# Column means of an 8192 x 8192 array: loads of 64 KB runs issued by GpSimd, and the last pieces through the SyncE queue

## Chip, cores and metric

One core of one Trainium2 chip. The metric is the device time of one execution in microseconds (us); lower is better.

## The reference

```python
"x": np.random.randn(8192, 8192).astype(np.float32)

def reference(x):
    return np.mean(x, axis=0)
```

268.4 MB are read once and 32 KB are written.

## The kernel before

Each row tile is 128 rows of 32 KB, one row per partition. One contiguous run of a load is called a descriptor here; the trace has one packet record for each (8064 of 32 KB for the 63 full tiles). TensorE multiplies it by a column of 1/8192, so that PSUM collects the column sums. Four row groups of 32 partitions in each of four PSUM banks hold the 16 blocks of 512 columns. The last 128 rows come in smaller pieces, so that little is left to do after the last byte.

```python
ld = tile_pool(name="ld", bufs=5)
for ri in range(n_rt - 1):                      # 63 tiles of 128 rows
    t = ld.tile([P, N], f32)
    nc.sync.dma_start(out=t[:], in_=x[ri * P:(ri + 1) * P, :])
    for b in range(NB):
        for q in range(4):
            c = (b * 4 + q) * F                 # F = 512
            mm(b, q, 0, F, t[:, c:c + F], ri == 0, False)
for b in range(NB - 1):                         # last 128 rows: three pieces of 1 MB
    t = lastp.tile([P, 4, F], f32, name=f"last{b}")
    nc.sync.dma_start(out=t[:], in_=x_v[r0:r0 + P, b])
    # 4 matmuls, copy from PSUM, store through ScalarE's queue
for s in range(F // SPL):                       # and four of 256 KB, runs of 512 B
    t = lastp.tile([P, 4, SPL], f32, name=f"lasts{s}")
    nc.sync.dma_start(out=t[:], in_=x_v[r0:r0 + P, b, :, s * SPL:(s + 1) * SPL])
    # 4 matmuls of 128 columns; after the last piece one copy and one store
```

## Time and profile before

| | before |
|---|---|
| time, median | 634.28 us |
| first input packet starts | 1.74 us |
| last input packet ends | 628.35 us |
| span (first to last instruction) | 632.6 us |

The rows in the middle are from the trace's packet records, which give each descriptor's queue, start, duration and size, but not its transfer engine. What is said of one engine is matched by time: 99% of the records of 32 KB, after the first 16, start within 4 ns of the end of another packet. The 626.6 us between them are a solid stream; 4.2 us follow it. The prediction shows the lines for this. Two more lines of the page matter later: the engines' busy times with their numbers of instructions, and the queue through which the core fetches its own instructions (packets, MB, share of the 16 engines).

```profile
PE 363.6 (57%) x2072; PEld 82.7 (13%) x2072; DVE 2.9 (0%) x5; POOL 0.2 (0%) x4
...
q8 instruction: 16, 0.26, 0.2%
```

The page has two records for each matmul of the program (2072 for 1036) and as many weight loads; numbers of matmuls here are the page's unless said otherwise. There are 16 instruction fetches of 16 KB.

### The profile page before, as it was taken

To read this page: it belongs to the slowest core of one execution; us is meant where nothing else is said; L and a number is where in the kernel's file an instruction comes from. 1 tells how busy PE (TensorE), PEld (TensorE's weight loads), DVE (VectorE), ACT (ScalarE), POOL (GpSimd) and SP (SyncE) were. 2 spreads that over 40 slices of the span, in tenths; PEclk is the share of its full clock that TensorE was granted. 3 is DMA by queue.
4 is the path that set the end of the run, shared out by engine and by line. 5 is a ranking of instruction groups with operands and counts; after the bars stand their busy time and mean duration, and the time that the engine had idled before them with its cause. 6 is when DMAs were issued, how large, how long until landed. Compare 5 with 4: busy or idle time off the path is not lost.

```text
span 632.6 us, 4331 instructions
## 1 busy us (share of the span) xinstructions
PE 363.6 (57%) x2072; PEld 82.7 (13%) x2072; DVE 2.9 (0%) x5; POOL 0.2 (0%) x4
## 2 busy tenths in 40 slices
PE   1564754656547546565476554655646646556466
PEld 0111111111111111111111111111111101111111
DVE  0000000000000000000000000000000000000001
POOL 0000000000000000000000000000000000000000
PEclk9868668667786686677866778668766686687767
DMA  9999999999999999999999999999999999999996
GB/s 371 433 440 437 432 431 431 428 431 430 431 433 430 431 430 433 431 432 431 430 431 431 428 434 430 431 431 430 433 428 431 431 430 431 432 435 430 431 427 233
DMA packets 11665, 268.74 MB, mean 425 GB/s; under 512 B 1136, under 2 KB 3184, under 8 KB 3200
## 3 DMA queue, kind: packets, MB, share of 16 engines
q1 hardware_dynamic: 11616, 268.44, 99.0%
q8 instruction: 16, 0.26, 0.2%
q10 hardware_dynamic: 32, 0.03, 0.0%
q14 instruction: 1, 0.01, 0.0%
HBM read 268.44 MB, written 0.03 MB: 424 GB/s over the span
## 4 chain that ended last, share of the span: by engine, by line
DMA 87%; PE 11%; SPq 1%; issue 0%; DVE 0%
DMA t<-in_x_dram 86%; PE bank L43 11%; DMA lasts<-in_x_dram 1%; SPq L76 1%; SPq L55 0%; DVE r L79 0%
## 5 line engine op out<-in xcount | busy, mean ns | idle before, releaser
L43 PE MATMUL bank<-t,ones 128*32 128x512 f32 x2016 | 359.8, 880 | 265.1 <-DMA t<-in_x_dram 265.1
L43 PEld LDWEIGHTS bank<-t,ones 128*32 128x32 f32 x2016 | 81.2, 153 | 542.5 <-DMA t<-in_x_dram 310.8
L70 DVE COPY r<-bank 128x512 f32<-128x512 f32 x3 | 2.1, 692 | 625.3 <-PE bank L43 625.3
L43 PE MATMUL bank<-last,ones 128*32 128x512 f32 x24 | 2.7, 592 | 0.0
L43 PE MATMUL bank<-lasts,ones 128*32 128x128 f32 x32 | 1.5, 279 | 0.5 <-DMA lasts<-in_x_dram 0.5
L43 PEld LDWEIGHTS bank<-last,ones 128*32 128x32 f32 x24 | 0.7, 110 | 2.2 <-issue 1.9
L43 PEld LDWEIGHTS bank<-lasts,ones 128*32 128x32 f32 x32 | 0.8, 109 | 1.6 <-DMA lasts<-in_x_dram 1.3
L79 DVE COPY r<-bank 128x512 f32<-128x512 f32 x1 | 0.7, 692 | 1.1 <-PE bank L43 1.1
L95 POOL MEMSET const-bfloat16-1.0<- 128x1 bf16 x1 | 0.1, 102 | 0.0
L95 POOL MEMSET const-uint8-127<- 128x1 uint8 x1 | 0.1, 102 | 0.0
L95 POOL MEMSET const-float32-0.0<- 128x1 f32 x1 | 0.1, 99 | 0.2 <-issue 0.2
L95 POOL MEMSET const-float32-1.0<- 128x1 f32 x1 | 0.1, 99 | 0.0
L39 DVE MEMSET ones<- 128x32 f32 x1 | 0.1, 85 | 0.8 <-PEq L95 0.8
## 6 DMA issues: line engine op xcount, KB each, us to landing
t<-in_x_dram SPq DMA_DIRECT2D x63, 4096.0 KB, 43.1
last<-in_x_dram SPq DMA_DIRECT2D x3, 1024.0 KB, 45.3
lasts<-in_x_dram SPq DMA_DIRECT2D x4, 256.0 KB, 19.1
out_dram<-r ACTq DMA_DIRECT2D x4, 8.0 KB
```

What stands on the lines that cost most here:

```text
L39: nc.vector.memset(ones[:], 1.0 / M)
L43: nc.tensor.matmul(out=banks[b][32 * q:32 * q + 32, c0:c0 + w], lhsT=ones[:], rhs=rhs, start=start, stop=stop, tile_position=(0, 32 * q), ...
L70: nc.vector.tensor_copy(out=r[:], in_=banks[b][:])
L76: nc.sync.dma_start(out=t[:], in_=x_v[r0:r0 + P, b, :, s * SPL:(s + 1) * SPL])
L79: nc.vector.tensor_copy(out=r[:], in_=banks[b][:])
L95: nc = _bacc.Bacc("TRN2", target_bir_lowering=False, num_devices=1)
```

## The change

The intent is to halve the number of descriptors: two neighbouring rows per partition make runs of 64 KB. GpSimd issues the loads of the first 31 tiles, each declared a single packet. The last 8 MB come in four pieces through SyncE's queue. The last 512 columns are summed by four matmuls of 128 columns into a PSUM tile of their own, so that the final copy is short.

```diff
-    for ri in range(n_rt - 1):
-        t = ld.tile([P, N], f32)                                   # bufs=5
-        nc.sync.dma_start(out=t[:], in_=x[ri * P:(ri + 1) * P, :])
-        # 16 matmuls of 512 columns
+    xt = x.rearrange("(t p j) c -> t p j c", p=P, j=2)
+    for ti in range(n_t - 1):                                      # 31 tiles of 256 rows
+        t = ld.tile([P, J, N], f32)                                # bufs=3
+        nc.gpsimd.dma_start(out=t[:], in_=xt[ti], single_packet=True)
+        for j in range(J):          # 15 matmuls of 512 columns and 4 of 128 ("edge")
+            sums(t, j, range(NBLK + 1), ti == 0 and j == 0, False)
-    # last 128 rows: 3 pieces of 1 MB, 4 of 256 KB
+    t = ld.tile([P, J, N], f32)
+    cuts = [(0, 8), (8, 12), (12, 15), (15, 16)]                   # blocks of 512 columns
+    for lo, hi in cuts:
+        nc.sync.dma_start(out=t[:, :, lo * F:hi * F], in_=xt[n_t - 1, :, :, lo * F:hi * F])
+    for lo, hi in cuts:
+        for j in range(J):
+            sums(t, j, range(lo, hi), False, j == J - 1)
+        # copies from PSUM and stores through ScalarE's queue, as before
```

(The store code and the index arithmetic are cut.)

More of the change, by code (lines that the diff above doesn't have):

```diff
@@ L27 @@
     F = 512
-    NB = N // (4 * F)
-    n_rt = M // P
-    SPL = 128
-    ld = ctx.enter_context(tc.tile_pool(name="ld", bufs=5))
-    lastp = ctx.enter_context(tc.tile_pool(name="lastp", bufs=1))
+    J = 2
+    NBLK = N // F - 1
+    W = F // 4
+    n_t = M // (P * J)
+    xt = x.rearrange("(t p j) c -> t p j c", p=P, j=J)
+    ld = ctx.enter_context(tc.tile_pool(name="ld", bufs=3))
     sg = ctx.enter_context(tc.tile_pool(name="sg", bufs=1))
@@ L39, with mm @@
     nc.vector.memset(ones[:], 1.0 / M)
-    banks = [psp.tile([P, F], f32, name=f"bank{b}") for b in range(NB)]
-    def mm(b, q, c0, w, rhs, start, stop):
+    banks = [psp.tile([P, F], f32, name=f"bank{b}") for b in range(4)]
+    edge = psp.tile([P, W], f32, name="edge")
+    def mm(dst, q, rhs, first, last):
         nc.tensor.matmul(
-            out=banks[b][32 * q:32 * q + 32, c0:c0 + w],
+            out=dst[32 * q:32 * q + 32, :],
             lhsT=ones[:],
             rhs=rhs,
-            start=start,
-            stop=stop,
+            start=first,
+            stop=last,
             tile_position=(0, 32 * q),
@@ L51, in mm @@
         )
-    for ri in range(n_rt - 1):
-        t = ld.tile([P, N], f32)
-        nc.sync.dma_start(out=t[:], in_=x[ri * P:(ri + 1) * P, :])
-        for b in range(NB):
-            for q in range(4):
-                c = (b * 4 + q) * F
-                mm(b, q, 0, F, t[:, c:c + F], ri == 0, False)
-    r0 = (n_rt - 1) * P
-    out_v = out.rearrange("(b q c) -> b q c", b=NB, q=4)
-    x_v = x.rearrange("r (b q c) -> r b q c", b=NB, q=4)
-    for b in range(NB - 1):
-        t = lastp.tile([P, 4, F], f32, name=f"last{b}")
-        nc.sync.dma_start(out=t[:], in_=x_v[r0:r0 + P, b])
-        for q in range(4):
-            mm(b, q, 0, F, t[:, q, :], False, True)
-        r = resp.tile([P, F], f32, name=f"r{b}")
-        nc.vector.tensor_copy(out=r[:], in_=banks[b][:])
-        nc.scalar.dma_start(out=out_v[b], in_=r[0:128:32, :])
@@ L72, with sums @@
-    b = NB - 1
-    r = resp.tile([P, F], f32, name=f"r{b}")
-    for s in range(F // SPL):
-        t = lastp.tile([P, 4, SPL], f32, name=f"lasts{s}")
-        nc.sync.dma_start(out=t[:], in_=x_v[r0:r0 + P, b, :, s * SPL:(s + 1) * SPL])
-        for q in range(4):
-            mm(b, q, s * SPL, SPL, t[:, q, :], False, s == F // SPL - 1)
-    nc.vector.tensor_copy(out=r[:], in_=banks[b][:])
-    nc.scalar.dma_start(out=out_v[b], in_=r[0:128:32, :])
+    def sums(t, j, blocks, first, last):
+        for i in blocks:
+            if i < NBLK:
+                mm(banks[i // 4], i % 4, t[:, j, i * F:(i + 1) * F], first, last)
+            else:
+                for q in range(4):
+                    c = i * F + q * W
+                    mm(edge, q, t[:, j, c:c + W], first, last)
@@ new lines @@
+    for ti in range(n_t - 1):
[10 more added lines that the diff above has]
+            sums(t, j, range(lo, hi), False, j == J - 1)
+        if hi <= NBLK:
+            for b in range(lo // 4, (hi + 3) // 4):
+                n = min(hi - 4 * b, 4)
+                r = resp.tile([P, F], f32, name=f"r{b}")
+                nc.vector.tensor_copy(out=r[:32 * n, :], in_=banks[b][:32 * n, :])
+                o = out[b * 4 * F:(b * 4 + n) * F].rearrange("(q c) -> q c", q=n)
+                nc.scalar.dma_start(out=o, in_=r[0:32 * n:32, :])
+        else:
+            r = resp.tile([P, W], f32, name="redge")
+            nc.vector.tensor_copy(out=r[:], in_=edge[:])
+            o = out[lo * F:hi * F].rearrange("(q c) -> q c", q=4)
+            nc.scalar.dma_start(out=o, in_=r[0:P:32, :])
```

## The prediction

> **What bounds the kernel now.** I read the page's row of slices first, then its chain, then the groups of instructions and the DMA issues, and last the end of the timeline.
>
> ```profile
> DMA  9999999999999999999999999999999999999996
> GB/s 371 433 440 437 432 431 431 428 431 430 431 433 430 431 430 433 431 432 431 430 431 431 428 434 430 431 431 430 433 428 431 431 430 431 432 435 430 431 427 233
> ...
> DMA packets 11665, 268.74 MB, mean 425 GB/s; under 512 B 1136, under 2 KB 3184, under 8 KB 3200
> ...
> DMA t<-in_x_dram 86%; PE bank L43 11%; DMA lasts<-in_x_dram 1%; SPq L76 1%; SPq L55 0%; DVE r L79 0%
> ...
> L43 PE MATMUL bank<-t,ones 128*32 128x512 f32 x2016 | 359.8, 880 | 265.1 <-DMA t<-in_x_dram 265.1
> ...
> t<-in_x_dram SPq DMA_DIRECT2D x63, 4096.0 KB, 43.1
> ```
>
> The transfer engines are busy in all forty slices and move some 431 GB/s in nearly every one; only the first (371) and last (233) fall short. The 11% for matmuls in the chain is no limit: the chain steps through TensorE because a free buffer lets the next load be issued, but each load has 43.1 us from issue to landing while one load's own share is 4.19 MB / 431 GB/s = 9.7 us. Four loads stand queued ahead of it, so a late release starves nothing. TensorE waits 265.1 us for loads.
>
> The end, from the timeline:
>
> ```profile
> 628.83 0.42 PE L43 MATMUL bank<-lasts,ones 128*32 128x128 f32 x8 [0.27 <-DMA lasts<-in_x_dram]
> 629.32 0.69 DVE L79 COPY r<-bank 128x512 f32<-128x512 f32 x1 [1.07 <-PE bank L43]
> 630.04 0.52 ACTq L80 DMA_DIRECT2D out_dram<-r  x1
> ```
>
> The last piece lands at about 628.8; eight matmuls, one copy and the store bring the span to 632.6, so the tail is 632.6 - 628.4 (last input packet, from the packet records) = 4.2 us. The first input packet starts at 1.7 us. Thus span = 1.7 (start) + 626.6 (transfer stream) + 4.2 (tail), and the timed 634.28 is 1.7 us above the span.
>
> Inside the 626.6 us I used the trace's packet records: each descriptor has its own record, and on one engine the next starts as the last ends. Start-to-start spacing, median: 32 KB 1213 ns (x504 per engine), 8 KB 309 ns (x24), 512 B 24 ns (x128), completion write 6 ns (x70). Sum: 611.4 + 7.4 + 3.1 + 0.4 = 622.3 us. The other 4.3 us are the slow first packets (1.8 to 2.1 us each), the 0.26 MB of instruction fetches and scattered stalls (the mean 32 KB spacing is 1218, not 1213). The slope between 8 KB and 32 KB is (1213 - 309) / 24576 B = 36.8 ps/B, that is 435 GB/s over 16 engines. What is left at 32 KB is 1213 - 32768 x 0.0368 = about 8 ns per descriptor (5 ns at 512 B). So the pure byte time of 268.4 MB is 617 us, and all that descriptor size can still win in the bulk is 504 x 8 ns = 4.0 us.
>
> [...]Before, issue at 0.73 and first packet at 1.7, 1.0 us; nothing in this trace shows the GpSimd path.
>
> **The change part by part.**
>
> *Descriptors of 64 KB.* Of 32 tiles of 8 MB, 31 go with 8 descriptors of 64 KB per engine: 248 per engine instead of 496 of 32 KB. If every descriptor still costs 8 ns: 248 x (65536 x 0.0368 + 8) = 248 x 2418 = 599.6 us. [...]Before, the same bytes took 496 x 1213 = 601.6 us. Gain 2.0 to 3.8 us.
>
> *Last tile in four pieces, two rows per partition.* Runs of 16, 8, 6 and 2 KB, 16 descriptors of each per engine: 16 x (611 + 309 + 234 + 83) = 19.8 us with the same slope plus 8 ns. Before, the same 256 rows took 8 x 1213 + 7.4 + 3.1 = 20.2 us. Gain 0.4 us, since 2048 runs of 512 B vanish. Completion writes fall from 70 to 35 per engine: 0.2 us.
>
> *GpSimd writes descriptors.* Between loads this lies beside the stream. A buffer falls free when TensorE has done 64 matmuls, about 2 x 6 us (a run of 32 is 5.0 to 6.6 us in the chain) after its tile landed; then two tiles of 19.5 us minus those 12 us are still queued, 27 us of cover. Only the first load's descriptor writing is exposed.[...]
>
> *Tail.* The last copy is 128x128 instead of 128x512 (0.69 us); an estimate is 0.3 us less. The last matmuls (eight of 128 columns) are the same number as before.
>
> Sum of the mechanism: -(2.0 to 3.8) - 0.4 - 0.2 + 1.0 - 0.3 = -1.9 to -3.7 us. A share of the scattered stalls (504 x 5 ns = 2.5 us) may go with the halved count of descriptors: about -1. That gives 629.6 to 631.4; I take 630.3.
>
> **The rivals.**
>
> *The last tile meets the GpSimd queue.* SyncE can issue its four pieces as soon as tile 28's buffer is free, about 12 us after tile 28 landed, while tile 29 is in flight and 30 is queued. If engines change queue only between packets, one small SyncE packet slips in and tile 30 still goes as one block; its 64 matmuls (11 to 13 us) then run under the last 19.7 us of pieces, and the pieces' 30 wide matmuls (30 x 0.19 = 5.7 us) just fit: 12 + 5.7 = 17.7 us. If instead 64 KB and 16 KB descriptors alternate, tile 30 lands later, with perhaps 13 us of pieces behind it or fewer; TensorE finishes 3 to 8 us after the last byte, and the time is 633 to 638. For it: engines do serve two queues at once here, since 16 KB instruction fetches took 1.0 to 1.1 us, longer than the 0.6 us of their bytes. [...]I give it one chance in five.
>
> [...]
>
> *Other read addresses.* Partitions step by 64 KB and not 32 KB. [...]A 1% loss gives 636; nothing in the profile speaks for it. One in fifteen.
>
> *All overhead goes and the start costs nothing.* 3.8 + 2.5 + 0.9 = 7.2 us less: 627. It is also nearly the floor: 617 + 1.7 + 4.2 + 1.7 = 624.6 at the slope's rate without any stall.
>
> **Range and chances.** The mechanism gives about 630 and its good end 627[...]. Faster by over 2% would be under 621.6, below that floor: 0.02. Slower by over 2% is over 647[...]: 0.05.
>
> **What would show it.** Right: slices at 432 to 434 GB/s; input descriptors of 64 KB spaced at 2410 to 2418 ns; half as many large packets; first input packet 1 us or so later; SyncE issues far before they land; last matmuls waiting for the last piece and not running behind. Wrong: a middle slice under 430 or gaps at tile borders[...]; TensorE busy without a break over the last 8 us with the last piece long landed (arbitration); slices above 435 (then the ceiling that I read from the slope is none).

The sum came to -1.9 to -3.7 us, and with about -1 for the stalls to 630.3 us. That engines change queue only between packets was the author's assumption, and the runs below show otherwise (103 packets of one queue to 106 of the other). "Two queues at once" is a reading of the fetches' duration that their starts and ends do not bear out. Of GpSimd's issues only the first stands in the chain afterwards, with 0.66 us.

## The result, and the profile after

638.75 us (637.68 to 639.12, 4 runs) against 634.4 (634.18 to 634.55, 4 runs, three of them those of the 634.28 above): ratio 1.0066, interval 1.0049 to 1.0083. By that ratio the change cost 4.2 us, where 4 us of gain were predicted.

The page after, the lines that answer to those of before: engines and instructions, slices, packets, queues, chain, issues.

```profile
PE 303.0 (48%) x2432; PEld 101.2 (16%) x2432; DVE 3.0 (0%) x6; POOL 16.7 (3%) x35
...
GB/s 391 399 458 411 441 457 408 448 407 445 453 415 441 420 436 437 433 436 432 429 436 421 449 428 436 421 440 433 428 449 411 453 415 441 424 433 442 410 415 86
DMA packets 5610, 268.79 MB, mean 422 GB/s; under 512 B 579, under 2 KB 583, under 8 KB 1110
...
q8 instruction: 19, 0.31, 0.2%
...
DMA t<-in_x_dram 75%; PE bank L47 17%; PE edge L47 2%; DVE r L83 0%; POOL t L68 0%; DVEq L116 0%; POOLq L105 0%
...
t<-in_x_dram POOLq DMA_DIRECT2D x31, 48.3
```

The packets are halved, as intended. The slices jump between 399 and 458 because a slice now counts few large packets; spread over each packet's duration, the records give 432 to 434 GB/s in every 20 us of the middle (mean 432.9), against 431 to 433 before (mean 431.2). So the bulk did get faster. The last slice is what stands out: 86 GB/s, where it was 233. The transfers end well before the kernel does. The timeline of TensorE, VectorE and ScalarE's issue near the end:

```profile
615.86 5.74 PE L47 MATMUL bank<-t,ones 128*32 128x512 f32 x27 [16.12 <-DMA t<-in_x_dram]
...
625.73 6.61 PE L47 MATMUL bank<-t,ones 128*32 128x512 f32 x56
...
632.60 0.61 PE L47 MATMUL edge<-t,ones 128*32 128x128 f32 x14
...
632.83 0.69 DVE L83 COPY r<-bank 96x512 f32<-96x512 f32 x1 [1.01 <-PE bank L47]
633.44 0.28 DVE L88 COPY redge<-edge 128x128 f32<-128x128 f32 x1
634.39 0.55 ACTq L90 DMA_DIRECT2D out_dram<-redge  x1
```

TensorE waits 16.12 us for tile 30, the last that GpSimd loads, and from 615.86 to 633.2 it doesn't wait for a transfer again: the bracket that names a wait is missing from every later group. The last input byte had landed at 627.7. SyncE's four issues stand far earlier, while tiles 29 and 30 were still moving:

```profile
578.28 2.57 SPq L75 DMA_DIRECT2D t<-in_x_dram  x4
```

In the packet records, tile 30's last 64 KB packet ended at 614.7, and by then 4.1 of the 8.4 MB of SyncE's pieces had landed. From 585 to 605 us, 103 packets of 64 KB and 106 of 16 KB started: the queues took turns, one descriptor for one.

The span splits as the prediction split it (us):

| | first input packet | stream | last byte to end | span |
|---|---|---|---|---|
| before | 1.74 | 626.6 | 4.2 | 632.6 |
| after | 2.62 | 625.1 | 9.6 | 637.3 |
| difference | +0.9 | -1.5 | +5.4 | +4.7 |

Two things had to be explained: the tail of +5.4, and why a bulk with half the descriptors gained only 1.5.

### The profile page after: what moved, and what is told of

Its sections match the earlier page's. It is cut to its first block, busy times and chain, and to the rows that moved or that the text cites. A ratio compares the mean times of both kernels' runs of the same rounds, so it can differ in the third digit from the quotient of the medians.

```text
span 637.3 us, 4993 instructions
## 1 busy us (share of the span) xinstructions
PE 303.0 (48%) x2432; PEld 101.2 (16%) x2432; DVE 3.0 (0%) x6; POOL 16.7 (3%) x35
## 4 chain that ended last, share of the span: by engine, by line
DMA 75%; PE 19%; another core or an unknown queue 4%; issue 1%; DVE 0%; POOL 0%; DVEq 0%; POOLq 0%
DMA t<-in_x_dram 75%; PE bank L47 17%; PE edge L47 2%; DVE r L83 0%; POOL t L68 0%; DVEq L116 0%; POOLq L105 0%
## 5 line engine op out<-in xcount | busy, mean ns | idle before, releaser
L47 PE MATMUL bank<-t,ones 128*32 128x512 f32 x1920 | 296.0, 738 | 330.2 <-DMA t<-in_x_dram 330.2
L47 PEld LDWEIGHTS bank<-t,ones 128*32 128x32 f32 x1920 | 87.3, 132 | 494.1 <-DMA t<-in_x_dram 314.4
L47 PE MATMUL edge<-t,ones 128*32 128x128 f32 x512 | 51.0, 277 | 0.0
L68 POOL DMA_DIRECT2D t<-in_x_dram x31 | 16.5, 532 | 542.3 <-PE edge L47 541.5
L47 PEld LDWEIGHTS edge<-t,ones 128*32 128x32 f32 x512 | 23.9, 110 | 37.7 <-issue 37.7
L83 DVE COPY r<-bank 128x512 f32<-128x512 f32 (+1 forms) x4 | 2.8, 691 | 629.9 <-PE bank L47 629.9
```

The costliest lines, as they stand in the source:

```text
L47: nc.tensor.matmul(out=dst[32 * q:32 * q + 32, :], lhsT=ones[:], rhs=rhs, start=first, stop=last, tile_position=(0, 32 * q), skip_group_ch ...
L68: nc.gpsimd.dma_start(out=t[:], in_=xt[ti], single_packet=True)
L83: nc.vector.tensor_copy(out=r[:32 * n, :], in_=banks[b][:32 * n, :])
```

## The experiments

All were timed in five rounds, except k in three. "Tail" is last input byte to end of span.

**a: the four pieces on GpSimd's queue.**

```diff
-        nc.sync.dma_start(out=t[:, :, lo * F:hi * F], ...
+        nc.gpsimd.dma_start(out=t[:, :, lo * F:hi * F], ...
```

> The last four pieces go through the GpSimd queue as well, behind tile 30. Theory T (engines take turns, one SyncE descriptor for one GpSimd descriptor, so tile 30 lands with only 13 us of transfers left while TensorE has 17 us of work): tile 30 lands some 4 MB earlier, near 605 us, TensorE waits for the last piece, tail back from 9.6 to about 4 us: 632 to 634 us. Rival R (the loss is in the stream: GpSimd descriptors or 64 KB runs let the engines drift apart): stays at 637 to 639.

634.78 us; 1.0006 of before (0.9994 to 1.0019), 4 us under the changed kernel. Tile 30 landed at 608.0 (before that only 1 MB of pieces), and the tail is 5.2 us. Its timeline:

```profile
608.56 5.77 PE L47 MATMUL bank<-t,ones 128*32 128x512 f32 x27 [9.85 <-DMA t<-in_x_dram]
...
623.33 1.92 PE L47 MATMUL bank<-t,ones 128*32 128x512 f32 x16 [1.26 <-DMA t<-in_x_dram]
...
627.02 1.49 PE L47 MATMUL bank<-t,ones 128*32 128x512 f32 x9 [1.77 <-DMA t<-in_x_dram]
```

TensorE waits for pieces again, up to the third of the four. The order of arrival was the cause of 4.4 of the 5.4 us by which the tail had grown. The time missed the expected 632 to 634 by 0.8 us: something else was still lost.

**b: without the single packet.**

```diff
-        nc.gpsimd.dma_start(out=t[:], in_=xt[ti], single_packet=True)
+        nc.gpsimd.dma_start(out=t[:], in_=xt[ti])
```

> As after, without the single packet. T: the packet flag does not hold the queue, turns are by descriptor anyway: within 1 us of after, 638 to 639.5, and the spacing of 64 KB descriptors stays 2416 to 2418 ns. If the flag held something back, SyncE's pieces now get a larger share while tile 29 and 30 are moving, and the time is 641 or more; if the flag saved per-descriptor cost, spacing rises by some ns and time by 1 to 2 us.

638.47 us (637.82 to 640.25), as with it. From 585 to 605 us 110 packets of 64 KB and 118 of 16 KB started, again in turn, and the 64 KB spacing is 2415 ns, against 2416. As used here the flag neither held the queue nor saved time.

**c: all tiles on SyncE's queue.**

```diff
-        nc.gpsimd.dma_start(out=t[:], in_=xt[ti], single_packet=True)
+        nc.sync.dma_start(out=t[:], in_=xt[ti])
```

> As after, with all tiles on the SyncE queue, 64 KB runs kept. T: order kept by the queue, TensorE not late, start 0.9 us earlier than with GpSimd: 631 to 633 us. Rival R in its form 'the 64 KB runs drift or read slower': 635 or more. This also says what 64 KB runs alone are worth against 634.4.

634.09 us; 0.9995 (0.9983 to 1.0008), which is not told apart from before. The first packet starts at 1.74 again, against 2.62 in after, so GpSimd's path costs 0.9 us once. But 631 to 633 us was missed by 1.1. The packet records say why. Each load ends with 16 completion writes (1120 records of 4 bytes for the 70 loads before), taken here as one for each of the 16 transfer engines. When all but the last 256 rows had landed (tile 30 here, the 62nd load before), these writes came on average at 604.1 us, against 606.1 before; the last of them came at 607.2, against 608.2. So the mean engine gained 2.0 us on the same bytes and the slowest 1.0. The last 256 rows then took the slowest engine 19.8 us instead of 20.2, and the last byte came 1.4 us earlier than before (627.0 against 628.3). The end of c:

```profile
626.18 1.49 PE L47 MATMUL bank<-t,ones 128*32 128x512 f32 x9 [1.80 <-DMA t<-in_x_dram]
...
627.61 0.93 PE L47 MATMUL edge<-t,ones 128*32 128x128 f32 x15
```

The matmuls of the last piece (edge) follow those of the third without a wait and end at 628.5, 1.6 us after the last byte; before it was 0.9 us (629.25 against 628.35).

**e: smaller first runs.** Same kernel as after, first piece cut into four (the copy of a bank then waits for both of its pieces; that edit isn't printed).

```diff
-    cuts = [(0, 8), (8, 12), (12, 15), (15, 16)]
+    cuts = [(0, 2), (2, 4), (4, 6), (6, 8), (8, 12), (12, 15), (15, 16)]
```

> As after (GpSimd tiles, SyncE pieces), but the first piece is cut into four with runs of 4 KB in place of 16 KB. T by descriptor turns: SyncE slips in 4 KB per 64 KB instead of 16 KB, so about 0.9 MB instead of 3 to 4 MB before tile 30 has landed; some 17 us of transfers are left then, TensorE is just in time: 633 to 635. If the engines shared by bytes or by time, 4 KB runs change nothing: 638 to 639. Rival R: 638 to 639.

635.51 us; 1.0016 (1.0004 to 1.0029). Half a microsecond above the expected window, but 3 us under the changed kernel. From 585 to 605 us, 115 packets of 64 KB and 139 of 4 KB started: still about one for one, though the bytes per turn fell to a quarter. That is a turn by descriptor, not by bytes or by time. Tile 30 landed at 609.7 after 1.9 MB of pieces, twice the 0.9 MB expected (why was not looked into), and the tail is 5.5 us.

*The second question: what holds some engines back.* A load's 16 completion writes show how far the engines have drifted apart. In the kernel before, the lags behind the first engine grow in steps: eight engines stay within 0.7 us throughout, and one engine after another of the other eight falls back by some 1.5 us. Each instruction fetch up to there starts within 4 ns of the end of a data packet and has a record of 1.0 to 1.1 us itself. As it ends (14 or 15 ns before), a data packet starts that is stretched by about 0.5 us (1680 to 1764 ns instead of 1216). Together that is 1.52 to 1.57 us for each of the 15 fetches, the size of a step. (The records name no engine; the match is by time.) Lags near the end of the bulk, and fetches up to then:

| kernel | fetches so far | lags of the slow eight, us | fetches per engine this suggests |
|---|---|---|---|
| before | 15 | one 1.6, seven 3.0 to 3.6 | 1 + 7 x 2 = 15 |
| c | 18 | six 3.0 to 3.3, two 5.0 to 5.1 | 6 x 2 + 2 x 3 = 18 |

So theory S, before the next runs: each fetch holds one engine up by 1.5 us, eight engines take them in turn, and the edge matmuls (2432 instead of 2072) brought some engines a third fetch.

**f: c without the edge matmuls.**

```diff
-            if i < NBLK:
-                mm(banks[i // 4], i % 4, t[:, j, i * F:(i + 1) * F], first, last)
-            else:
-                for q in range(4):
-                    c = i * F + q * W
-                    mm(edge, q, t[:, j, c:c + W], first, last)
+            mm(banks[i // 4], i % 4, t[:, j, i * F:(i + 1) * F], first, last)
```

The last copy then takes 32x512 of bank 3.

> c with the last 512 columns summed by one matmul like the others instead of four of 128 columns: 2048 matmuls instead of 2432, so 16 instruction fetches instead of 18 or 19. Theory S: each 16 KB fetch of instructions holds up one transfer engine by about 1.5 us, they fall in turn on eight engines, and the engine with the most fetches (three in c, lag 5.0 us) ends the stream. Then no engine has a third fetch: last input byte 1 to 1.5 us earlier than in c (627.0), time 632.6 to 633.5 with a last copy up to 0.5 us longer. Rival D (64 KB runs let the engines drift by themselves): lag of 5 us and time as in c, 634.1 or a little more.

16 fetches; largest lag at tile 30 3.5 us (15 fetches so far: seven of 3.0 to 3.5, one of 1.8). The last byte lands at 625.9, 1.1 us earlier than in c, as S has it. Yet the time is 634.29 (1.0000, 0.9988 to 1.0013), because my mended tail was worse: 6.6 us. Its end:

```profile
627.12 0.69 DVE L77 COPY r<-bank 96x512 f32<-96x512 f32 x1 [3.01 <-PE bank L46]
...
627.86 1.90 PE L46 MATMUL bank<-t,ones 128*32 128x512 f32 x4 [0.80 <-DVE r L77]
...
629.80 0.70 DVE L82 COPY redge<-bank 32x512 f32<-32x512 f32 x1 [2.00 <-PE bank L46]
```

With the edge in the same bank, the last matmuls wait for the copy of that bank (the bracket names VectorE). That is what the separate edge tile had bought.

**g: c with VectorE adding the two rows first.**

```diff
-        for j in range(J):
-            sums(t, j, range(NBLK + 1), ti == 0 and j == 0, False)
+        for k in range(4):
+            h = slice(k * 4 * F, (k + 1) * 4 * F)
+            nc.vector.tensor_add(out=t[:, 0, h], in0=t[:, 0, h], in1=t[:, 1, h])
+            sums(t, 0, range(4 * k, 4 * k + 4), ti == 0, False)
```

> c with VectorE adding the two rows of each partition in the first 31 tiles, so TensorE needs 627 matmuls instead of 2432, some 5 fetches. S: no engine has more than one fetch, largest lag about 1.5 to 2 us instead of 5.0 at tile 30, last input byte 2 to 3.5 us earlier than in c: 630.5 to 632 us. D: lag and time as in c, 634. A third possibility: VectorE's adds[...] hold buffers longer and the stream gets gaps: over 635.

632.60 us; 0.9972 (0.9960 to 0.9985): faster than both kernels. The page:

```profile
PE 220.1 (35%) x1254; PEld 35.5 (6%) x1254; DVE 278.9 (44%) x130; POOL 0.2 (0%) x4
...
q8 instruction: 10, 0.16, 0.1%
```

I had mixed two counts: 627 are the program's matmuls, which is 1254 of the page's, and so there are 10 fetches, not 5. Nine had come by tile 30, where eight engines lag by 1.1 to 1.8 us and one by 2.6. S accounts for 7 + 2 = 9 of these steps; one of the eight lags remains without a fetch (one packet at 262.1 us was stretched by 0.6 us with no fetch beside it). The last byte lands at 625.1, 1.9 us earlier than in c. The miss of 0.6 us against the expected range fits the five fetches too few in my count, since one engine got a second one; no run separates this.

**h: the changed kernel with the same adds.** Edit as in g, on the changed kernel.

> The changed kernel itself (GpSimd tiles, single packet, SyncE pieces) with the same VectorE adds. T: SyncE still takes turns, tile 30 still lands near 615, but now some 9 us of VectorE and 7 us of trailing TensorE work overlap and end by about 626, so little or nothing is late: tail about 5 us instead of 9.6; with S the stream also ends 2 to 3 us earlier: 631 to 634 us. If turns cost transfer time in themselves: 636 or more.

636.40 us; 1.0033 (1.0019 to 1.0047): a miss. The stream ended 1.4 us earlier than in the changed kernel (626.3 against 627.7), as S says, but the tail is still 8.4 us. I had counted VectorE's and TensorE's work as overlapping to the end. Its chain of waits shows that they don't:

```profile
613.77 4.50 DVE t L71 x2
618.28 0.04 issue
618.32 5.51 PE bank L47 x29
...
624.15 5.29 PE bank L47 x44
```

Tile 30 landed at 612.6; its four adds lasted from 613.77 to 622.7 (8.9 us, where some 9 were expected), TensorE could end it only after the last of them, and the pieces' matmuls followed without a wait, to 630.2. From landing to end these are again some 17 us of work against 13.7 us of transfers left, so the long tail stays. The turns themselves cost little transfer time: the stream is 0.3 us longer than g's (623.7 against 623.4).

**i and k: the kernel before with matmuls of half width,** so twice the instructions and nothing else.

```diff
-                mm(b, q, 0, F, t[:, c:c + F], ri == 0, False)
+                for h in (0, F // 2):
+                    mm(b, q, h, F // 2, t[:, c + h:c + h + F // 2], ri == 0, False)            # i
+                    mm(b, q, h, F // 2, t[:, c + h:c + h + F // 2], ri == 0 and h == 0, False) # k
```

> The kernel before with matmuls of 256 columns instead of 512 in the 63 full tiles: 4088 matmuls instead of 2072, 31 or 32 instruction fetches instead of 16, nothing else. S: up to four fetches on each of eight engines, lag 6 to 7 us instead of 3.6 before the last pieces, time 634.4 + 2.5 to 3.5 = 637 to 638. If a fetch costs only the 0.6 us of its bytes: 635.5 to 636. D: 634.4.

i took 637.38 us, but its result was wrong (relative error 0.089), which was not meant. An error of 0.088 would come of losing the first 128 of 8192 rows in half of the columns, the square root of 1/64 x 1/2 (an estimate for random input).

> i gave a wrong result, since the start flag of the second half column block undid the first half's first sum; here only the first half starts a sum. Same instruction count: S expects the same time as i, 637.4 us (3.0 over before), a largest lag near 6.7 us before the last pieces, and a right result. If i's time had to do with its error: 634 to 635.

k, whose only difference from i is the start flag of the second halves, is right and takes 637.25 us (637.21 to 637.36); 1.0047 (1.0033 to 1.0061), 3.0 us over the 634.24 of before.

```profile
PE 354.6 (56%) x4088; PEld 186.9 (29%) x4088; DVE 2.9 (0%) x5; POOL 0.2 (0%) x4
...
q8 instruction: 32, 0.52, 0.3%
```

TensorE is no busier than before (354.6 us against 363.6). With 30 fetches so far, six engines lag by 6.3 to 6.6 us and two by 4.5 to 5.0: 6 x 4 + 2 x 3 = 30. The last byte lands 2.8 us later. Two more fetches on the slowest engines at 1.5 us each are 3.0: doubling the instructions and nothing else gives the step that S asks for.

**j: g with the last store issued by SyncE.**

```diff
-            nc.scalar.dma_start(out=o, in_=r[0:P:32, :])     # of the edge
+            nc.sync.dma_start(out=o, in_=r[0:P:32, :])
```

> g with the last store (2 KB) issued by SyncE, which is idle then, instead of ScalarE, which in g is still issuing the store before it: 0.67 us lay between the end of the last copy and the issue. Expected 0.4 to 0.7 us less than g's 632.6: 632.0 to 632.2, the best so far. If the end is set by the store before the last, no change: 632.6.

632.26 us; 0.9969 (0.9955 to 0.9982). 0.34 us less than g: a little less gain than expected, and small beside the runs' spread of 0.5. It was run at another time. It is the lowest of all kernels here: 2 us under before, 6.5 under the changed kernel.

## Why the prediction was wrong

- **The step that failed is the choice between the packet and the descriptor as the unit of turns.** The prediction called "64 KB and 16 KB descriptors alternate" a rival, gave it one chance in five (b shows no effect of the flag), and built its point on tile 30 going "as one block", with a tail of 3.9 us (4.2 - 0.3). The runs show turns by descriptor, with and without the flag (103 to 106; b 110 to 118). Half of the pieces (4.1 of 8.4 MB) came before the end of tile 30, and the tail was 9.6 us. The rival's own numbers held or nearly: "perhaps 13 us of pieces behind it" was 13.0 (614.7 to 627.7), TensorE's 17.7 us of work was 17.3 (615.86 to 633.2), and the time, "633 to 638", was 638.75. Order restored, a gets 4.0 us of it back. The trace before held a hint that was read otherwise: the prediction took the fetches' 1.0 to 1.1 us for two queues served at once, but each fetch starts as one data packet ends (within 4 ns), and another starts as it ends (14 to 16 ns before). Matched by time, an engine changed queue between two descriptors there too.
- **Gain of the bulk.** 64 KB spacing of "2410 to 2418 ns": 2416, so two former descriptors (2426) are 10 ns cheaper. The 2.0 to 3.8 us for the descriptors (2.0 is 601.6 - 599.6; b shows no gain by the flag) hold at their low end for the mean engine (2.0, from c), not for the slowest (1.0), and it is the slowest that ends the stream. The 0.4 us for the last tile came (20.2 to 19.8).
- **A term left out: instructions.** The prediction counted 64 matmuls per tile. The page has 76 (two for each of 38), since the edge takes four instead of one; 19 fetches instead of 16 put a third fetch on some engines. The "scattered stalls" that it hoped to shrink with the descriptors were in good part these fetches: 15 of 1.57 us over 16 engines are some 1.5 of the 2.5 us (an estimate from the two figures). f, g and k show the fetches' cost from three sides. Why a fetch costs 1.5 us, when a data packet of the same 16 KB took 0.61 (after), is not shown.
- **Start.** The 1.0 in the sum was 0.9: GpSimd's first issue began 0.5 us later (1.25 us in after, 0.73 in c), and from issue to first packet it took 1.4 us instead of 1.0.
- **Tail without the lateness.** "0.3 us less" was 0.9 us more (c: 5.17 against 4.25). Some 0.7 us of it are the matmuls, which end 1.6 us after the last byte instead of 0.9, because the last piece lands while TensorE is still at the third. The other 0.3 us come after them: the short copy of 0.28 us stands behind a 0.69 us copy and its store behind another store; j got 0.34 back there. No run changed the first part.

## What to carry to other kernels

When two queues are at work at once, count what each delivers per turn. Here work queued early on SyncE delayed GpSimd's last tile: tile 30 landed at 614.7 us, after half of the pieces, and at 608.0 in a, which puts the bytes that are needed last behind the others on one queue and is 4 us faster. In these streams the slowest engine set the end, and instruction fetches counted there at about 1.5 us each. So fewer instructions shortened a kernel whose compute engine had time to spare (g against c: 10 fetches instead of 19, the last byte 1.9 us earlier). Gains of 1% in such a stream were to be read from the completion of each engine, not from the mean rate: in c the mean engine gained 2.0 us and the slowest 1.0.
